# All subtractions for low parts put on VectorE, and a new model of the engines in the clock that orders a four-mixer encoder

## The chip, the cores and the metric

One core of one Trainium2 chip runs the whole program. The metric is device time in microseconds (us); lower is better. The engines are TensorE (PE in the profile, its weight loads PEld), VectorE (DVE), ScalarE (ACT), GpSimd (POOL) and SyncE (SP, which here only issues transfers).

## The reference

Two residual layers over 1024 tokens of width 1024. In each layer one input projection feeds four causal token mixers, each is gated and projected back, the four are merged by sigmoid gates, and an output projection closes the layer:

```python
h = _rmsnorm(x, norm_w)
p = h @ w_in                       # 1024 -> all inputs, gates of the four branches included
u_a = _rwkv7_branch(...)           # RWKV-7: state recurrence with a rank-one removal per token
u_b = _retention_branch(...)       # retention: chunked decay attention
u_c = _ssd_branch(...)             # Mamba-2 SSD: convolution, then chunked decay attention
u_d = _gdn_branch(...)             # gated DeltaNet: convolution, then a triangular solve per chunk
merged = sum(gates[:, :, b] * (u_b_ @ w_branch[b]) for b, u_b_ in enumerate((u_a, u_b, u_c, u_d)))
x = x + merged @ w_out
```

After the second layer comes a last RMSNorm. Everything is float32.

## The kernel before

The work goes in four passes: two layers, each over two halves of 512 tokens. Weights come in slabs of 128 x 512 values (912 in all). A product keeps float32 accuracy with TensorE's faster format `fp32r` by splitting both operands into a high part H (the value cast to `fp32r`) and a low part L (the value minus H): each block of a slab is used for H·H, H·L and L·H, so a slab of four blocks is 12 matmuls of 512 columns. The cast of a slab (`hl<-raw`, ACT or DVE) is made up to three slabs ahead of its use, and the subtraction (also `hl<-raw,hl`) up to two slabs ahead; `split` and `low` emit them, `prefetch` calls them when a slab is taken. The same subtraction gives the L parts of the normalised input (`hL`), of the branches' results (`u`, `acc`, `lo`) and of small operands of the RWKV-7 and DeltaNet units (`w`, `GE`, `GF`).

`subtract` decides which engine makes an L part:

```python
def sooner(self, a, b, n, what=""):
    ck = self.ck
    return ck.t[a] + ck.cost(a, what, n) <= ck.t[b] + ck.cost(b, what, n) + 0.8

def subtract(self, out, a, b):
    e = self.nc.gpsimd if self.sooner("gpsimd", "vector", int(np.prod(out.shape[1:]))) else self.nc.vector
    e.tensor_tensor(out, a, b, ALU.subtract)
```

Each pass runs 12 units (pieces of the mixers: `ret`, `gdn`, `ssd`, `rw`), every one a chain of short steps that go back and forth between PE and the other engines. Beside them runs the stream of big products (input projection, merges, gates, output projection), which needs nothing of the chains for most of its length. The program is one straight list of instructions, and each engine takes its own in the order in which they were emitted. That order is set when the program is built, by `Clock`, an estimate of when each engine gets to what is emitted: `Clock.cost` has a price for every instruction, `Clock.op` adds it after what the instruction reads or overwrites is over, and the loop in `mixers` emits a unit's next step as soon as the clock's PE time has reached the step's ready time, and otherwise a piece of the stream of products:

```python
now = ck.t["pe"]
for t in sorted(self.tasks, ...):
    if t.ready > now:
        continue
    ck.step = now
    r = next(t.gen, "end")             # emit one step of a unit
    ...
    t.ready = ck.step + ck.HAND        # the next step: after all this one emitted is over
    break
else:
    r = next(fill, "end") if more else None   # emit a piece of a product
```

So where the clock takes an engine for faster than it is, a unit's product stands too early in PE's queue, and PE, which takes its instructions in order, stands still there.

The chains that matter here are the inverses of unit lower triangular matrices (`inverse`, 12 per pass: 4 of `gdn`, 8 of `rw`). One inverse begins on DVE with the diagonal blocks (`invw<-GA,con` or `invw<-GE,con`, four instructions), a reduction and three or four instructions `GR<-invw,con`. Then PE spreads them (`m<-GR,con`, the first matmul of an inverse), DVE solves the small blocks in some twenty short dependent instructions (`invw<-m,invw`, `invw<-invw`, 4 to 64 elements), and five to eight rounds of PE and DVE double the blocks (`m<-invw,GA`, `m<-invw,GE`, `m<-invw`). The scores from which `GA` is made are `m<-w,w` and `m<-GE,w`. In the convolution (`ev_conv`, units `gdn` and `ssd`) DVE runs three instructions `cvy<-cvraw,par,cvy` and one `in<-cvraw,cvy` for each block of 128 channels.

Names in the profile: `g` are PSUM banks of the big products, `m` and `y` those of the units; `raw` and `hl` a slab as it comes and its H and L parts; `hH`/`hL`/`u` activations; `invw`, `GR`, `GA`, `GD`, `GE`, `GF`, `w` the units' working tiles; `rs` roots on POOL. All instructions of DVE, ACT and POOL have the line of the recording helper, L365 (L387 after the change), and PE has L438 for a matmul and L442 for a transpose (L465 and L469), so one goes by the tiles' names.

Of the kernel before, what the change touches and what calls it, by code (L numbers as in the profile page):

```python
# [16 lines left out]
P = 128  # L17
D = 1024
S = 1024
T = 512          # tokens per pass  # L20
NC = 4           # chunks per pass
C = 128          # tokens per chunk
# [5 lines left out]
# units in the order in which a pass runs them  # L28
# [3 lines left out]
# what a unit takes from the input projection, in the order of the products, with its place in memory; what has two  # L32
# places is 256 columns wide and has the tokens in the partitions
# [11 lines left out]
# The products of a pass in the order in which the tensor engine takes them, between the steps of the units.  # L45
# "out" is the output projection of the pass before, "norm" the normalisation of the input of the next pass;
# the last branch is merged in two steps, gates and projections.
# [4 lines left out]
# the first pass  # L52
# [10 lines left out]
# the others  # L63
# [36 lines left out]
def slabs_of(it):  # L100
    """The slabs of weights of an item of the plan, each of four blocks of 128 rows and 128 columns, or of two of
    128 rows and 256 columns."""
    if it[0] in ("sm", "lora", "out"):
        return [it + (e,) for e in range(2)]
    if it[0] == "in":
        return [("in",) + UNITS[it[1]] + (it[2], e) for e in range(2 * len(ROLES[UNITS[it[1]][0]][it[2]]))]
    if it[0] == "merge":
        b = BRANCH[it[1]]
        return [("gate", b, it[2], 0), ("gate", b, it[2], 1), ("proj", b, it[2])]
    b = BRANCH[MERGES[-1]]  # L110
    return {"gate": [("gate", b, it[-1], 0), ("gate", b, it[-1], 1)], "proj": [("proj", b, it[-1])], "norm": []}[it[0]]
# [7 lines left out]
def sequence(npass):  # L119
    """The items of the plan for all passes, each with its pass."""  # L120
# [32 lines left out]
# columns of the packed small parameters  # L153
# [10 lines left out]
def ssd_blk(idx, role):  # L164
    """Index of a 128-wide block of xbc."""
# [46 lines left out]
# constants: name -> (first column, width)  # L212
# [10 lines left out]
def make_consts():  # L223
# [42 lines left out]
    rope = np.stack([ct, st, ct * sc, st * sc])          # 4, P, S  # L266
# [4 lines left out]
class Clock:  # L271
    """An estimate, in microseconds, of when the engines get to what is emitted; it orders the steps."""
    HAND = 0.2       # from one engine to another

    def __init__(self):
        self.t = {e: 0.0 for e in ("pe", "vector", "scalar", "gpsimd", "dma")}
        self.slot, self.owner, self.written, self.read = {}, {}, {}, {}
        self.step = 0.0

    def place(self, tile, key):  # L280
        """The tile lies where the last one with this key lay."""
        self.slot[tile] = key
        self.owner[key] = tile

    def grains(self, ap):
        """Pieces of 128 elements of a tile's place which an operand touches; a bank of PSUM counts as one, as its
        users take turns."""
# [12 lines left out]
    def op(self, eng, outs, ins, cost):  # L300
        at = self.t[eng]
        gi, go = [g for a in ins for g in self.grains(a)], [g for a in outs for g in self.grains(a)]
        for g in gi:
            w = self.written.get(g)
            if w:
                at = max(at, w[0] + (0.13 if w[1] == eng else self.HAND))
        for g in go + [g for g in gi if g[1] < 0]:
            for d in (self.written, self.read):
                w = d.get(g)
                if w and w[1] != eng:  # L310
                    at = max(at, w[0] + self.HAND)
        end = self.wait(eng, at) + cost
        for g in gi:
# [10 lines left out]
    def settled(self, *aps):  # L324
        """When the last writes to these operands are over."""
# [6 lines left out]
    def cost(self, eng, name, n):  # L332
        if eng == "vector":
            return 0.07 + n * (0.52e-3 if name == "copy" else 1.04e-3)
        if eng == "scalar":
            return 0.1 + n * 0.83e-3
        return {"memset": 0.1 + n * 0.83e-3, "tensor_copy": 0.2 + n * 3.4e-3, "affine_select": 0.2 + n * 0.85e-3,
                "pow": 0.4 + n * 0.165}.get(name, 0.2 + n * 1.97e-3)


class Engine:
    """An engine whose instructions the clock sees."""
# [4 lines left out]
    def __getattr__(self, what):  # L347
        fn = getattr(self.real, what)

        def call(*a, **k):  # L350
# [8 lines left out]
            else:  # L359
                nm = "pow" if ALU.pow in a else what  # L360
                if what == "tensor_copy" and self.name == "vector" and not any(x.tensor.name.split("_")[0] in "mgy" for x in ops):
                    nm = "copy"
                self.clock.op(self.name, outs, [x for x in ops if not any(x is o for o in outs)],
                              self.clock.cost(self.name, nm, n))
# [11 lines left out]
def finish(gen):  # L376
    """What the generator returns, after all its steps."""
# [12 lines left out]
class Trunk:  # L390
# [12 lines left out]
    # ---------------------------------------------------------------- tiles  # L403
# [29 lines left out]
    # ---------------------------------------------------------------- tensor engine, with its time kept  # L433
    def mm(self, out, lhsT, rhs, **k):
        n, m = (int(np.prod(ap.shape[1:])) for ap in (rhs, lhsT))
        cost = (2 if m > 64 else 1.2) * max(n, m, 16) * 0.84e-3 if rhs.dtype == F32 else max(n, 64) * 0.42e-3
# [3 lines left out]
    def tr(self, out, in_, ident):  # L440
        self.ck.op("pe", [out], [in_], max(out.shape[-1], in_.shape[-1]) * 0.84e-3)
        self.nc.tensor.transpose(out, in_, ident)  # L442

    # ---------------------------------------------------------------- set-up
    def setup(self):
        nc = self.nc
        # schedule state
# [48 lines left out]
    def derive(self, l):  # L496
        """What follows from the parameters alone."""
# [14 lines left out]
    # ---------------------------------------------------------------- weights  # L512
# [4 lines left out]
    def prefetch(self, g):  # L517
        """Loads up to slab g + 5; H parts up to slab g + 3, L parts up to slab g + 2."""
# [4 lines left out]
    def split(self, high, low):  # L523
        """H parts of the slabs up to high, L parts of those up to low."""
# [25 lines left out]
    def flush(self):  # L550
        """The last steps of what takes the products out of PSUM."""
# [4 lines left out]
    def sooner(self, a, b, n, what=""):  # L556
        """Whether engine a is done sooner with an instruction over n elements than engine b."""
        ck = self.ck
        return ck.t[a] + ck.cost(a, what, n) <= ck.t[b] + ck.cost(b, what, n) + 0.8

    def subtract(self, out, a, b):
        e = self.nc.gpsimd if self.sooner("gpsimd", "vector", int(np.prod(out.shape[1:]))) else self.nc.vector
# [15 lines left out]
    def slab_gemm(self, rhs, evac):  # L578
        """The next slabs of weights, as H + L, against rhs, pairs of H and L of blocks of 128 rows."""
# [17 lines left out]
    def narrow_gemm(self, rhs, evac):  # L597
        """The like for 16 columns, which the slabs have twice: H and L parts side by side."""
# [13 lines left out]
    def wide_gemm(self, lhs, evac):  # L612
        """The like with the tokens in the partitions, for slabs of 256 columns; a bank has two chunks."""
# [23 lines left out]
    # ---------------------------------------------------------------- norm  # L637
# [3 lines left out]
    def squares(self, acc, k, x, tags=("w5", "w6")):  # L641
        """acc (+)= x^2"""
# [7 lines left out]
    def rms_rows(self, *accs, tag="w7"):  # L650
        """[P, T] tile with rsqrt(mean(x^2) + eps) of each token in every partition; accs have the squares' sums
        over the blocks of 128 features."""
# [20 lines left out]
    def wt(self, i):  # L673
        """A tile in the working memory of the units, free when none of them runs."""
# [50 lines left out]
    # ---------------------------------------------------------------- input blocks  # L725
    def ev_shift(self, ps, l, muix, mu, out, hf):
        """Token shift: out = t * (1 - mu) + previous(t) * mu."""
# [12 lines left out]
    def ev_conv(self, ps, l, cvix, wname, wix, bias, out, hf, done):  # L740
        """Causal convolution of four taps, then 2 * silu."""
# [26 lines left out]
    def ev_silu(self, ps, out):  # L768
        """out = 2 * silu(ps)."""
# [4 lines left out]
    def unit_input(self, l, hf, kind, idx, role, io):  # L774
        """One of the blocks of 128 columns of the input projection which a unit takes."""
# [43 lines left out]
    def small(self, l, hf):  # L819
        """dt, beta and alpha of every head: decays, their running sums and what follows from them."""  # L820
# [9 lines left out]
    def decays(self, l, hf, s):  # L830
# [17 lines left out]
        # log(1 + e) = 2 atanh(e / (2 + e))  # L848
# [33 lines left out]
    def lora(self, l, hf):  # L882
        """The narrow inputs of RWKV-7, with the H part in one half of the partitions and the L part in the other."""
# [15 lines left out]
    # ---------------------------------------------------------------- merge  # L899
    def h_gemm(self, evac, gemm=None):  # L900
        """The next slabs against the normalised input; at the start against what is not yet scaled."""
# [53 lines left out]
    # where the gates of the last branch wait: in working memory, and in the places of inputs  # L955
# [1055 lines left out]
```

## Time and profile before

| | before |
|---|---|
| time, median of 3 runs | 3782.73 us (3783.42, 3778.8, 3782.73) |
| span of the profiled execution | 3775.2 us |
| its own time | only the span is given; the runs lie 3.6 to 8.2 us above it |
| PE busy | 3577.6 us (95%) |
| DVE busy | 2543.6 us (67%) |
| POOL busy | 1790.6 us (47%) |
| ACT busy | 1401.4 us (37%) |
| transfers | 295.48 MB, mean 78 GB/s |

How to read it: the span runs from the first to the last instruction. A matmul's busy time is modelled and matmuls overlap, so PE's 95% isn't PE at its peak; what counts for PE is the time in which it stands still, what ended each of these waits, and the granted clock (1.0 is full speed). On the other engines idle time costs nothing by itself.

### The profile page before, as it was taken

The numbers are of one execution on the slowest core, as the hardware profiler recorded it, in microseconds if no ns is written. First come the engines' busy times: TensorE is split into PE (matmuls) and PEld (weight loads), VectorE is DVE, ScalarE is ACT, GpSimd is POOL, SyncE is SP. The second block draws the span as 40 slices with busy tenths as digits, with TensorE's granted clock in tenths as the row PEclk, the third lists the DMA queues.
The fourth block names the chain that finished last, engine by engine and source line by source line (L and its number), as shares of the span: only waits on it lengthen the run. The fifth ranks groups of instructions, "written<-read, shape, count | busy, mean of one in ns | idle before, by whom it ended". The sixth has DMA issues, their size and how long they took to land. (4 is left out here: it accounts for less than half of the span.)

```text
span 3775.2 us, 66152 instructions
## 1 busy us (share of the span) xinstructions
PE 3577.6 (95%) x24904; PEld 2864.7 (76%) x24904; DVE 2543.6 (67%) x5607; ACT 1401.4 (37%) x3121; POOL 1790.6 (47%) x1846
## 2 busy tenths in 40 slices
PE   7999999999999999999999999999999999999998
PEld 5777877777877787777787778777778778867777
DVE  6678666766577856567657775757665876675664
ACT  4433343333243334333324334433332433443333
POOL 4534554545453445445545445444454534454444
PEclk9999999999999999999999999999999999999999
DMA  3212222113322222212332222221243222221124
GB/s 121 72 59 65 73 72 61 52 60 114 124 76 79 65 73 68 61 54 71 113 126 75 71 73 70 62 64 55 71 125 113 86 64 68 70 65 58 57 76 148
DMA packets 162176, 295.48 MB, mean 78 GB/s; under 512 B 17984, under 2 KB 21440, under 8 KB 161856
## 3 DMA queue, kind: packets, MB, share of 16 engines
q1 hardware_dynamic: 150192, 271.22, 24.1%
q10 hardware_dynamic: 11664, 20.02, 1.6%
q8 instruction: 197, 3.23, 0.4%
q14 instruction: 123, 1.01, 0.1%
HBM read 280.69 MB, written 10.49 MB: 77 GB/s over the span
## 5 line engine op out<-in xcount | busy, mean ns | idle before, releaser
L438 PE MATMUL g<-hH,hl 128*128 128x512 f32 (+1 forms) x5176 | 1773.9, 415 | 8.4 <-DVE cvraw L365 4.9
L365 POOL TENSOR_TENSOR hl<-raw,hl 128x512 fp32r<-128x512 f32 x700 | 960.6, 1377 | 745.0 <-ACT hl L365 659.2
L438 PEld LDWEIGHTS g<-hH,hl 128*128 128x128 f32 (+1 forms) x5176 | 974.9, 191 | 240.5 <-issue 10.3
L438 PE MATMUL g<-hL,hl 128*128 128x512 f32 x2600 | 1040.8, 400 | 0.0
L365 ACT CAST hl<-raw 128x512 fp32r<-128x512 f32 x851 | 521.8, 618 | 684.4 <-PE g L438 270.0
L438 PE MATMUL g<-u,hl 128*128 128x512 f32 (+1 forms) x2112 | 608.9, 411 | 24.1 <-ACT hH L365 9.7
L438 PEld LDWEIGHTS g<-hL,hl 128*128 128x128 f32 x2600 | 496.8, 191 | 113.0 <-issue 8.6
L438 PEld LDWEIGHTS g<-u,hl 128*128 128x128 f32 (+1 forms) x2112 | 391.5, 191 | 122.3 <-ACT hH L365 12.2
L365 POOL TENSOR_TENSOR rs<-rs,mhalf 128x4 f32<-128x4 f32 (+2 forms) x80 | 106.5, 1331 | 401.5 <-DVE rs L365 401.2
L365 DVE SCALAR_TENSOR_TENSOR cvy<-cvraw,par,cvy 128x512 f32<-128x512 f32 x244 | 257.7, 1056 | 41.8 <-ACT cvy L365 30.4
L365 DVE TENSOR_TENSOR hl<-raw,hl 128x512 fp32r<-128x512 f32 x212 | 211.5, 1007 | 27.4 <-ACT hl L365 26.3
L438 PE MATMUL g<-hl,hH 128*128 128x256 f32 x1024 | 190.0, 285 | 2.7 <-DVE hl L365 2.7
L365 DVE TENSOR_TENSOR invw<-invw 128x4 f32<-128x4 f32 (+3 forms) x464 | 164.3, 354 | 15.9
L365 ACT COPY cvraw<-g 128x512 f32<-128x512 f32 (+1 forms) x160 | 93.5, 585 | 187.5 <-PE g L438 145.6
L438 PEld LDWEIGHTS g<-hl,hH 128*128 128x128 f32 x1024 | 160.3, 191 | 3.6 <-DVE hl L365 2.9
L365 POOL TENSOR_SCALAR_AFFINE_SELECT GA<-GA 128x512 f32<-128x512 f32 x128 | 85.2, 672 | 121.8 <-ACT GA L365 121.8
L365 ACT ACTIVATE cvraw<-cvy 128x512 f32<-128x512 f32 x80 | 50.2, 628 | 234.9 <-DVE cvy L365 217.2
L365 POOL TENSOR_TENSOR acc<-acc,tg 128x512 f32<-128x512 f32 x64 | 90.3, 1411 | 81.4 <-DVE tg L365 70.6
L438 PE MATMUL g<-hl,hL 128*128 128x256 f32 x512 | 125.6, 283 | 0.0
L438 PE MATMUL m<-w,w 64*128 64x256 f32 (+1 forms) x640 | 115.5, 312 | 1.3 <-ACT w L365 0.5
L365 ACT ACTIVATE tg<-g 128x512 f32<-128x512 f32 x100 | 59.6, 596 | 150.1 <-PE g L438 109.1
L365 ACT ACTIVATE in<-g 128x512 f32<-128x512 f32 x84 | 49.3, 597 | 169.2 <-PE g L438 169.2
(340 smaller groups left out, 5682.2 us busy)
## 6 DMA issues: line engine op xcount, KB each, us to landing
raw<-W SPq DMA_DIRECT2D x912, 256.0 KB, 2.6
w<-x ACTq DMA_DIRECT2D x32, 256.0 KB, 3.5
tg<-rope SPq DMA_DIRECT2D x16, 256.0 KB, 3.0
cvy<-rope SPq DMA_DIRECT2D x16, 256.0 KB, 3.4
w<-x SPq DMA_DIRECT2D x16, 256.0 KB, 4.4
x<-tg ACTq DMA_DIRECT2D x12, 256.0 KB, 2.1
x<-cvy ACTq DMA_DIRECT2D x12, 256.0 KB, 2.0
GA<-xT SPq DMA_DIRECT2D x8, 256.0 KB, 5.1
```

The source lines that it names most:

```text
L365: return fn(*a, **k)
L438: self.nc.tensor.matmul(out, lhsT, rhs, **k)
```

## The change

Three things change; tables of the order of products, tiles and arithmetic stay, and comments are dropped.

1. `subtract` always takes VectorE.
2. The clock knows a port that VectorE and GpSimd share: an instruction for which `ported` holds (all of GpSimd's that read, and on VectorE `tensor_tensor`, `scalar_tensor_tensor` and copies whose operands all lie in SBUF, and longer `tensor_scalar`) starts only when the port is free and holds it to its end. `sooner` looks at the port too.
3. Prices change: a `fp32r` matmul of 512 columns from 0.215 to 0.233 us, small float32 matmuls by their tile, GpSimd's copies and selections, a surcharge for `scalar_tensor_tensor` and for a sum written beside an activation.

```diff
-    def op(self, eng, outs, ins, cost):
+    def op(self, eng, outs, ins, cost, port=False):
...
+        if port:
+            at = max(at, self.port)
         end = self.wait(eng, at) + cost
+        if port:
+            self.port = end
...
-        return {"memset": 0.1 + n * 0.83e-3, "tensor_copy": 0.2 + n * 3.4e-3, "affine_select": 0.2 + n * 0.85e-3,
-                "pow": 0.4 + n * 0.165}.get(name, 0.2 + n * 1.97e-3)
+        return {"memset": 0.1 + n * 0.83e-3, "tensor_copy": 0.13 + n * 1e-3, "affine_select": 0.1 + n * 0.95e-3,
+                "pow": 0.4 + n * 0.15}.get(name, 0.2 + n * 1.97e-3)
+
+    def ported(self, eng, name, ins):
+        if eng == "scalar" or not ins or any(self.slot.get(x.tensor.name, ("",))[0] in ("m", "g", "y") for x in ins):
+            return False
+        return eng == "gpsimd" or name in ("tensor_tensor", "scalar_tensor_tensor", "tensor_copy", "copy") \
+            or (name == "tensor_scalar" and int(np.prod(ins[0].shape[1:])) >= 32)
+
+    def free(self, eng, port=False):
+        return max(self.t[eng], self.port) if port else self.t[eng]
...
+                if port and what == "scalar_tensor_tensor":
+                    c += n * 0.12e-3
+                if self.name == "scalar" and k.get("accum_out") is not None:
+                    c += 0.15
...
-        cost = (2 if m > 64 else 1.2) * max(n, m, 16) * 0.84e-3 if rhs.dtype == F32 else max(n, 64) * 0.42e-3
+        if rhs.dtype != F32:
+            cost = max(n, 128) * 0.456e-3
+        elif m <= 64:
+            cost = 0.03 if m <= 32 else 0.11 if n <= 64 else n * 1.7e-3
+        else:
+            cost = 2 * max(n, m) * 0.85e-3
...
-        return ck.t[a] + ck.cost(a, what, n) <= ck.t[b] + ck.cost(b, what, n) + 0.8
+        at = {e: ck.free(e, e != "scalar") + ck.cost(e, what, n) for e in (a, b)}
+        return at[a] <= at[b] + 0.8
...
-        e = self.nc.gpsimd if self.sooner("gpsimd", "vector", int(np.prod(out.shape[1:]))) else self.nc.vector
+        e = self.nc.vector
```

In the built program the counts are: PE 19362 matmuls before and now; DVE 5609 and 6514; POOL 1851 and 910; ACT 3044 and 3079; SP 1045 and 1045. From POOL to DVE go 940 subtractions: 700 of slabs (`hl<-raw,hl`, 912 of 912 are now on DVE), 86 others of 512 elements and 154 of 256, and one scaling at the end. 37 casts of slabs go from DVE to ACT.

First place: DVE's queue where the first group of the second `rw` unit of the first pass begins its inverse. `GD` to `GE` are the operands of another group's scores, `hl` are slabs. Before:

```order
L365 SCALAR_TENSOR_TENSOR GD_6_6252<-in_10_4896,par_67,w_7_5514 128x2x128
L365 TENSOR_TENSOR GD_6_6252<-in_10_4956,w_7_5514 128x2x128
L365 TENSOR_TENSOR GF_7_6259<-w_11_5736,GF_7_6259 128x256
L365 TENSOR_TENSOR GE_7_6258<-GD_6_6252,w_13_6257 128x512
L365 TENSOR_TENSOR invw_4_6268<-GA_7_6102,con_81 32x128 x4
L365 TENSOR_REDUCE invw_4_6268<-invw_4_6268 128x32
L365 TENSOR_TENSOR GR_6_6103<-invw_4_6268,con_81 128x64
```

Now:

```order
L387 TENSOR_TENSOR hl_6179<-raw_6092,hl_6179 128x512
L387 SCALAR_TENSOR_TENSOR GD_6_6252<-in_10_4876,par_67,w_7_5571 128x2x128
L387 TENSOR_TENSOR GD_6_6252<-in_10_4938,w_7_5571 128x2x128
L387 TENSOR_TENSOR w_15_6255<-w_13_5732,w_15_6255 128x256
L387 TENSOR_TENSOR w_12_6256<-w_9_5737,w_12_6256 128x256
L387 TENSOR_TENSOR GF_7_6259<-w_11_5739,GF_7_6259 128x256
L387 TENSOR_TENSOR GE_7_6258<-GD_6_6252,w_13_6257 128x512
L387 TENSOR_TENSOR invw_4_6268<-GA_7_6102,con_81 32x128 x4
L387 TENSOR_REDUCE invw_4_6268<-invw_4_6268 128x32
L387 TENSOR_TENSOR GR_6_6103<-invw_4_6268,con_81 128x64
```

The slab's and two `w` subtractions, which stood on POOL, now stand on DVE ahead of the inverse; from `GE` on the rows are the same.

Second place: PE's queue where the first `gdn` inverse of the second pass begins with `m<-GR,con` (128x480). `g` rows are the stream of products, `hl_` the slab. Before:

```order
L438 MATMUL g_10747<-hH_8995,hl_10639 128x512 x4
L438 MATMUL g_10747<-hH_8995,hl_10666 128x512
L438 MATMUL g_10747<-hL_8996,hl_10666 128x512
L438 MATMUL m_10782<-GR_10_10527,con_81 128x480
L438 MATMUL g_10747<-hH_8995,hl_10666 128x512
```

Now:

```order
L465 MATMUL g_10795<-hH_8995,hl_10738 128x512 x4
L465 MATMUL g_10839<-hH_8995,hl_10757 128x512
L465 MATMUL g_10839<-hL_8996,hl_10757 128x512
L465 MATMUL m_10847<-GR_10_10532,con_81 128x480
L465 MATMUL g_10839<-hH_8995,hl_10757 128x512
```

The inverse's first product has moved back in PE's queue by three slabs, 36 matmuls of 512 columns (`hl_10685` and `hl_10738` stand in between).

Third place: POOL's queue in the first pass, where an `rw` unit's state is carried from chunk to chunk (`sf`, `sh`). Before:

```order
L365 MEMSET sh_6848 128x128
L365 TENSOR_TENSOR sf_6885<-sh_6848,fc_5603 128x128
L365 TENSOR_TENSOR hl_6837<-raw_6744,hl_6837 128x512
L365 MEMSET sh_6916 128x128
L365 TENSOR_TENSOR rs_9_6929<-rs_9_6929,mhalf_89 128x4
L365 TENSOR_TENSOR hl_6899<-raw_6791,hl_6899 128x512
L365 TENSOR_TENSOR sf_6973<-sh_6916,fc_5603 128x128
```

Now:

```order
L387 TENSOR_TENSOR sf_6902<-sh_6278,fc_5651 128x128
L387 MEMSET sh_6944 128x128
L387 TENSOR_TENSOR sf_6965<-sh_6944,fc_5651 128x128
L387 MEMSET sh_6981 128x128
L387 TENSOR_TENSOR rs_9_6994<-rs_9_6994,mhalf_89 128x4
```

No subtraction is left on POOL; its other work stands as before.

More of the change, by code (lines that the diff above doesn't have):

```diff
@@ L273 @@
     HAND = 0.2
+    SAME = 0.13
     def __init__(self):
@@ L278, in __init__ @@
         self.step = 0.0
+        self.port = 0.0
     def place(self, tile, key):
@@ L305, in op @@
             if w:
-                at = max(at, w[0] + (0.13 if w[1] == eng else self.HAND))
+                at = max(at, w[0] + (self.SAME if w[1] == eng else self.HAND))
         for g in go + [g for g in gi if g[1] < 0]:
@@ L362, in call @@
                     nm = "copy"
-                self.clock.op(self.name, outs, [x for x in ops if not any(x is o for o in outs)],
-                              self.clock.cost(self.name, nm, n))
+                ins = [x for x in ops if not any(x is o for o in outs)]
+                c, port = self.clock.cost(self.name, nm, n), self.clock.ported(self.name, what, ins)
+                if port and what == "scalar_tensor_tensor":
+                    c += n * 0.12e-3
+                if self.name == "scalar" and k.get("accum_out") is not None:
+                    c += 0.15
+                self.clock.op(self.name, outs, ins, c, port)
             return fn(*a, **k)
@@ L440, in tr @@
     def tr(self, out, in_, ident):
-        self.ck.op("pe", [out], [in_], max(out.shape[-1], in_.shape[-1]) * 0.84e-3)
+        self.ck.op("pe", [out], [in_], max(out.shape[-1], in_.shape[-1]) * 0.86e-3)
         self.nc.tensor.transpose(out, in_, ident)
```

## Prediction

> **What bounds the kernel now.** I read the page's head first, then the waits of PE, then one long wait as a timeline, then the rows of the tiles in it. The page and the list of cores:
>
> ```profile
> span 3775.2 us, 66152 instructions
> PE 3577.6 (95%) x24904; PEld 2864.7 (76%) x24904; DVE 2543.6 (67%) x5607; ACT 1401.4 (37%) x3121; POOL 1790.6 (47%) x1846
> core 0: 3775.2 us, clock 0.978
> ```
>
> PE stands still for 3775.2 − 3577.6 = 198 us. The granted clock of 0.978 costs 3775.2 x 0.022 = 83 us more. The rest is matmul work that the change doesn't touch, so at most 281 us can go, and some of that belongs to the start and the end. Who ends PE's waits (us in total, times, longest):
>
> ```profile
> PE m L438 <- DVE invw L365: 77.3, 62, 2.7
> PE m L438 <- DVE GR L365: 13.8, 10, 3.6
> PE m L438 <- DVE GE L365: 12.9, 18, 1.5
> PE m L438 <- DVE stgdn L365: 11.0, 14, 1.9
> PE g L438 <- ACT hH L365: 9.7, 6, 2.4
> PE m L438 <- DVE yB L365: 8.9, 4, 3.4
> PE m L442 <- DVE GA L365: 6.3, 15, 1.1
> PE g L438 <- POOL hl L365: 2.3, 7, 0.5
> ```
>
> Steps of the units that DVE has not finished end most of it: the first four rows alone are 115.0 us. The slabs' L parts on POOL (last row) are no bottleneck themselves. Why DVE is late shows the timeline at the first place of the order (start, duration, engine; the bracket is the idle time before):
>
> ```profile
> 662.24 1.77 DVE L365 TENSOR_TENSOR GE<-GD,w 128x512 fp32r<-128x512 f32 x1
> 663.42 1.72 POOL L365 TENSOR_TENSOR hl<-raw,hl 128x512 fp32r<-128x512 f32 x1
> 663.94 2.61 DVE L365 TENSOR_TENSOR invw<-GA,con 32x128 f32<-32x128 f32 x4
> 664.07 0.39 PE L438 MATMUL m<-GE,w 64*128 64x256 f32 x1 [0.64 <-DVE GE L365]
> 665.55 0.39 PE L438 MATMUL g<-hL,hl 128*128 128x512 f32 x1
> 666.59 0.38 DVE L365 TENSOR_REDUCE invw<-invw 128x32 f32<-128x128 f32 x1
> 667.00 1.48 DVE L365 TENSOR_TENSOR GR<-invw,con 128x64 f32<-128x64 f32 x3
> 667.02 1.32 POOL L365 TENSOR_TENSOR hl<-raw,hl 128x512 fp32r<-128x512 f32 x1
> 668.62 0.45 PE L438 MATMUL m<-GR,con 128*128 128x112 f32 x2 [2.68 <-DVE invw L365]
> ```
>
> While a slab's subtraction runs on POOL, DVE's instructions with two inputs in SBUF stretch: four short ones take 2.61 us, three others 1.48 us. PE has run out of the products put ahead of `m<-GR,con` at 665.94 and waits 2.68 us. The tiles' rows (minimum, median, maximum in ns; then two groups with busy time and mean) say the same for all passes:
>
> ```profile
> L365 DVE TENSOR_TENSOR invw<-GA,con x128: 268/289/1362, 562.5 to 3636.5; 32x128 f32<-32x128 f32 x128
> L365 DVE TENSOR_TENSOR GR<-invw,con x160: 160/218/1357, 190.9 to 3637.5; 128x64 f32<-128x64 f32 x48, 128x32 f32<-128x32 f32 x48, 128x16 f32<-128x16 f32 x32, 128x256 f32<-128x256 f32 x16
> L365 DVE TENSOR_TENSOR invw<-invw x464: 166/168/1349, 198.4 to 3644.8; 128x4 f32<-128x4 f32 x87, 128x8 f32<-128x8 f32 x41, 128x16 f32<-128x16 f32 x23, 128x32 f32<-128x32 f32 x4
> L365 DVE TENSOR_TENSOR invw<-invw 128x4 f32<-128x4 f32 (+3 forms) x464 | 164.3, 354 | 15.9
> L365 DVE SCALAR_TENSOR_TENSOR cvy<-cvraw,par,cvy x244: 750/752/1710, 138.0 to 3243.6; 128x512 f32<-128x512 f32 x122
> L365 DVE SCALAR_TENSOR_TENSOR cvy<-cvraw,par,cvy 128x512 f32<-128x512 f32 x244 | 257.7, 1056 | 41.8 <-ACT cvy L365 30.4
> L365 POOL TENSOR_TENSOR hl<-raw,hl x700: 1256/1297/2267, 4.7 to 3752.0; 128x512 fp32r<-128x512 f32 x175
> ```
>
> Medians are clean, means and maxima are not: the longest `invw<-invw` is 168 ns plus about one POOL subtraction. In the solve of one inverse the loss is 464 x (354 − 168) ns / 48 inverses = 1.8 us, near the long waits at `m<-invw`.
>
> **The change part by part.** What leaves POOL is 15 groups. The largest and the smallest of them, ACT's cast of a slab, three instructions that follow each other on DVE (from the timeline), and the longest undisturbed run of products (from the chain of work that ended last):
>
> ```profile
> L365 POOL TENSOR_TENSOR hl<-raw,hl 128x512 fp32r<-128x512 f32 x700 | 960.6, 1377 | 745.0 <-ACT hl L365 659.2 <-DVE hl L365 52.7 <-PE m L438 16.6
> L365 POOL TENSOR_TENSOR lo<-tg,u 128x512 fp32r<-128x512 f32 x1 | 1.3, 1309 | 1.3 <-ACT u L365 1.3
> L365 ACT CAST hl<-raw 128x512 fp32r<-128x512 f32 x851 | 521.8, 618 | 684.4 <-PE g L438 270.0 <-issue 121.7 <-DMA raw<-W 109.6
> 742.36 0.41 DVE L365 TENSOR_TENSOR GD<-in,w 128x256 f32<-128x256 f32 x1
> 742.69 0.68 DVE L365 TENSOR_TENSOR hl<-raw,hl 128x512 fp32r<-128x512 f32 x1
> 743.29 0.15 DVE L365 TENSOR_TENSOR invw<-m,invw 128x4 f32<-128x4 f32 x1
> 3414.33 25.25 PE g L438 x108
> ```
>
> All 15 together are 1215 us, so POOL keeps about 575 us, 32% of its time. On DVE a subtraction occupies the queue from its start to the next start: 743.29 − 742.69 = 0.60 us for 512 elements, 742.69 − 742.36 = 0.33 us for 256. So DVE takes on 786 x 0.60 + 154 x 0.33 = 522 us; the 37 casts that leave it only lower that. It gets back, from the two rows of excess shown above, 244 x (1056 − 752) + 464 x (354 − 168) ns = 160 us, of which POOL's 68% is 109 us, and more from rows not shown. A subtraction also waits for its cast, and on DVE everything behind it waits along:
>
> ```profile
> L365 DVE TENSOR_TENSOR hl<-raw,hl 128x512 fp32r<-128x512 f32 x212 | 211.5, 1007 | 27.4 <-ACT hl L365 26.3
> ```
>
> The 212 already on DVE stood 26.3 us for ACT, 0.12 us each (on POOL 659.2 us, where nothing urgent was behind); 700 more make 87 us.
>
> The terms for PE, against the span:
>
> A. The four rows of 115.0 us. At 668.6 the clean chain is 4 x 0.29 + 0.38 + 3 x 0.22 = 2.2 us from 663.94 and ends at 666.1, 0.2 us after PE's products: the wait of 2.68 us shrinks to that. The slab's and the two `w` subtractions, now ahead of `GE` on DVE, cost 1.26 us there, but delay the scores `m<-GE,w` and the inverse alike. At the second place `m<-GR,con` also stands 36 matmuls of 25.25/108 = 0.234 us, 8.4 us, further back, for a wait of at most 3.6 us. As 32% of POOL's time stays to collide with, I take two thirds of the row: −77 us. Ends: 0 (the subtractions on DVE are as much in the way as POOL was) and −115.
>
> B. The other rows of DVE (`yB`, `GA`: 15.2 us): half, −8; ends 0 and −15. ACT's rows and the start stay.
>
> C. The clock. The stretch right behind the wait at 668.6 (length, then busy time of PE, PEld, DVE, ACT and POOL; the granted clock stands third from the end):
>
> ```profile
> 669.10:672.50 3.40, 3.40 (x13) 2.39 (x14) 2.85 (x17) 1.10 (x2) 0.00 (x0) 0.50 0.28 77
> ```
>
> After a wait of 2.68 us PE gets half speed for 3.4 us, which costs 1.7 us more. The 83 us shrink with the waits, by (77 + 8)/198: −36 us; ends 0 and −65. The Trainium skill, "TensorE: Matmul & The Clock Gate", section "HAM oscillation — how this bites in real kernels", puts the limit at idle gaps over about 3.4 us, by which this term would be near 0 and the sum −65. The trace disagrees: 2.68 us was enough, and the row decides.
>
> D. What gets in the way anew. The subtractions and their waits take (522 + 87)/3775 = 16% of DVE's time. The order has 48 inverses with 7 or 9 groups of products, 400 in all; if each meets half a subtraction (0.30 us) with that probability and nothing covers it, that is 400 x 0.16 x 0.30 = 19 us: +20. Ends: 0, and 400 x 0.30 = +120 if each one meets one.
>
> Costed at nothing: the casts on ACT (37 x 0.618 = 23 us; ACT is 37% busy and sits 684 us idle before such casts; a slab is cast three slabs of 12 x 0.234 = 2.8 us ahead; without that cover 23 us). A slab's L part is due two slabs, 5.6 us, ahead; if DVE's queue is longer than that, PE waits on `hl`, and the slab's `raw` buffer comes free later, so that SP issues the next load later: between 0 and +20, I take 0, since the longest block, a convolution's, is 3 x 0.75 us. POOL's roots `rs` and states `sf` lose the subtractions ahead of them; DVE has room for these waits, so no gain is counted.
>
> Sum: −77 − 8 − 36 + 20 = −101 us. The profiled span lies 7.5 us below the median of the runs; 3782.7 − 101 = 3682 us.
>
> **The rivals.** *Slower, because DVE becomes the bound.* Three stretches of 95 us (PE, PEld, DVE, ACT, POOL busy), then the part of slabs' tiles in the first:
>
> ```profile
> 1995.00:2090.00 95.00, 89.27 (x488) 71.10 (x487) 80.72 (x163) 43.39 (x118) 54.30 (x48) 0.96 0.27 82
> 2945.00:3040.00 95.00, 85.67 (x559) 66.91 (x558) 81.57 (x193) 42.23 (x110) 45.55 (x46) 0.98 0.25 81
> 1900.00:1995.00 95.00, 94.60 (x493) 77.74 (x492) 51.17 (x102) 27.39 (x57) 39.49 (x30) 1.00 0.37 117
> 1995.00:2090.00 95.00, 80.61 (x324) 60.47 (x323) 4.89 (x3) 15.88 (x26) 34.37 (x24) 0.96 0.27 82
> ```
>
> In the convolutions DVE is already at 81 of 95 us; 24 subtractions more are +14.4, which is full unless the contention goes. Between the second and third row PE loses 8.9 us for 30.4 us more of DVE, 0.29 per us. If DVE ends 300 us busier over all (522 less twice the relief counted above), that is +87: 3870 us. It decides from the point at which a convolution stretch stays above some 90 of 95 us. Against it: the same rows' POOL time falls by 34 of 54 us, and `cvy` alone loses 0.3 us a piece in contention. *Little, because the places only change.* The port is held by DVE's own subtractions instead of POOL's, and the order gains a third of A and C: about −40, 3740 us. The Trainium skill, "Perfetto Trace Analysis", section "Optimizing Scalar/DVE Operations", says that moving work between GpSimd and DVE might not help, as they share a port. Against it stand 1.297 us on POOL for 0.60 on DVE. *No change*, if D eats all of A to C: 3783. *Nearly all goes*: A, B and C at their ends, D 0: −195, 3588 us.
>
> **How the numbers follow.** The forecast case (3635 to 3730) 0.45; little (3730 to 3775) 0.22; nearly all (3560 to 3635) 0.15; no change 0.05; slower 0.13. The skill's rule on the clock has 0.03 of the forecast's chance, and its 3718 lies inside. A change within 0.2% (7.6 us) can't be told from none; so faster 0.82, same 0.05, slower 0.13. For 8 in 10 the range goes from 3575 to 3785: it leaves out nearly all of slower and the lowest tail of the gain.
>
> **What the profile after would show.** POOL near 575 us, `hl<-raw,hl` x912 on DVE with a mean near 0.75 us, `invw<-invw` well under 354 ns, `cvy` under 900: contention gone. DVE at 2700 to 2950 us: D and the relief. PE's waits for `invw`, `GR`, `GE`, `stgdn` under 50 us in all and a clock of 0.985 or more: A and C. I am wrong if PE's waits for `hl`, `hH` or `u` grow by tens of us, or if DVE's contention with what stays on POOL (roots, selections, sums) keeps the inverses as long as they are.

## The result, and the profile after

| | before | changed kernel |
|---|---|---|
| median of the runs (lowest to highest) | 3783.07 us (3778.8 to 3791.84, 4 runs) | 3702.70 us (3700.13 to 3705.72, 4 runs) |
| ratio, 95% interval | | 0.978 [0.9762, 0.9798] |
| profiled execution: span | 3775.2 us | 3703.7 us |
| PE busy, PE standing still | 3577.6, 197.6 us | 3553.5, 150.2 us |

The kernel became 80 us faster; 101 had been forecast. The profiled execution of before was one of the quicker ones and that of the changed kernel the slowest of its four, so the two traces differ by 71.5 us. The head of the page, after:

```profile
span 3703.7 us, 65695 instructions
PE 3553.5 (96%) x24904; PEld 2854.5 (77%) x24904; DVE 2595.0 (70%) x6512; ACT 1427.2 (39%) x3156; POOL 600.5 (16%) x905
```

And the list of cores, with the granted clock (0.978 before):

```profile
core 0: 3703.7 us, clock 0.981
```

POOL lost 1190 us of work, DVE won 905 instructions and yet only 51 us. The reason stands in the groups of DVE (busy time, mean ns of one, then the idle time ahead of them):

```profile
L387 DVE TENSOR_TENSOR hl<-raw,hl 128x512 fp32r<-128x512 f32 x912 | 667.8, 740 | 42.4 <-ACT hl L387 39.7
L387 DVE SCALAR_TENSOR_TENSOR cvy<-cvraw,par,cvy 128x512 f32<-128x512 f32 x244 | 186.7, 765 | 56.2 <-ACT cvy L387 46.8 <-issue 0.5
L387 DVE TENSOR_TENSOR invw<-invw 128x4 f32<-128x4 f32 (+3 forms) x464 | 83.6, 180 | 15.9
```

and in the tile's row (minimum, median, maximum in ns):

```profile
L387 DVE TENSOR_TENSOR invw<-invw x464: 166/168/721, 190.7 to 3574.6; 128x4 f32<-128x4 f32 x87, 128x8 f32<-128x8 f32 x41, 128x16 f32<-128x16 f32 x23, 128x32 f32<-128x32 f32 x4
```

The means have come down to the medians: 354 to 180 ns in the inverses, 1056 to 765 ns in the convolutions, 1007 to 740 ns in the slabs' own subtraction. The longest `invw<-invw` is 721 ns instead of 1349. That DVE itself was no slower before is shown by a neighbour of these instructions in the same chain, which has one of its two inputs in PSUM (`m`) and not in SBUF. Its row before and after:

```profile
L365 DVE TENSOR_TENSOR invw<-m,invw x480: 122/164/292, 198.2 to 3644.6; 128x4 f32<-128x4 f32 x88, 128x16 f32<-128x16 f32 x40, 128x64 f32<-128x64 f32 x24, 128x128 f32<-128x128 f32 x8
L387 DVE TENSOR_TENSOR invw<-m,invw x480: 122/164/293, 190.5 to 3574.4; 128x4 f32<-128x4 f32 x88, 128x16 f32<-128x16 f32 x40, 128x64 f32<-128x64 f32 x24, 128x128 f32<-128x128 f32 x8
```

It never stretched: its longest is 292 ns with POOL busy for 47% of the time and 293 with 16%. The same steps as at the first place of the order, in the timeline of after:

```profile
638.09 0.68 DVE L387 TENSOR_TENSOR GE<-GD,w 128x512 fp32r<-128x512 f32 x1
638.69 1.17 DVE L387 TENSOR_TENSOR invw<-GA,con 32x128 f32<-32x128 f32 x4
640.32 0.41 DVE L387 TENSOR_TENSOR GR<-invw,con 128x64 f32<-128x64 f32 x3
641.00 0.37 PE L465 MATMUL m<-GR,con 128*128 128x112 f32 x2
```

The four short ones take 1.17 us (2.61 before), the three others 0.41 (1.48), and PE takes `m<-GR,con` without a wait (2.68 before). The rest of the gain's story is in PE's waits (total us, times, longest):

```profile
PE g L465 <- DVE hl L387: 48.1, 33, 7.4
PE m L465 <- DVE invw L387: 18.6, 25, 3.6
PE m L465 <- ACT w L387: 17.1, 6, 3.4
PE g L465 <- DVE cvraw L387: 11.7, 7, 2.4
PE m L465 <- DVE yC L387: 8.7, 3, 3.0
PE m L465 <- DVE GE L387: 2.4, 6, 0.6
PE m L465 <- DVE GR L387: 2.0, 3, 0.7
PE m L469 <- DVE yB L387: 1.9, 2, 1.7
```

The four rows that led before, 115.0 us, are 23.0 us (`stgdn` has no row any more). At the top stands a wait for slabs' L parts. It had been 7.0 us: the 2.3 us of POOL's row and this one:

```profile
PE g L438 <- DVE hl L365: 4.7, 3, 2.7
```

The longest wait for `hl` after, in the timeline:

```profile
1101.18 0.40 PE L465 MATMUL g<-acc,hl 128*128 128x512 f32 x1
1103.07 0.68 ACT L387 ACTIVATE cvy<-g,par 128x512 f32<-128x512 f32 x1
1103.78 3.03 DVE L387 SCALAR_TENSOR_TENSOR cvy<-cvraw,par,cvy 128x512 f32<-128x512 f32 x3 [1.13 <-ACT cvy L387]
1106.90 0.63 ACT L387 ACTIVATE cvraw<-cvy 128x512 f32<-128x512 f32 x1 [3.16 <-DVE cvy L387]
1107.44 1.12 ACT L387 CAST hl<-raw 128x512 fp32r<-128x512 f32 x2
1107.64 0.69 DVE L387 SCALAR_TENSOR_TENSOR in<-cvraw,cvy 128x512 f32<-128x512 f32 x1 [0.83 <-ACT cvraw L387]
1108.25 1.29 DVE L387 TENSOR_TENSOR hl<-raw,hl 128x512 fp32r<-128x512 f32 x2
1108.99 1.22 PE L465 MATMUL g<-u,hl 128*128 128x512 f32 x2 [7.40 <-DVE hl L387]
```

A convolution goes from ACT to DVE, back to ACT and to DVE again, each waiting for the other (1.13, 3.16 and 0.83 us in the brackets). The cast of the next slab stands behind it in ACT's queue and the subtraction behind it in DVE's. Both engines are idle at times, but neither can take the slab first, and PE has no products left at 1101.6. What that wait costs beyond itself is shown by the granted clock (third from the end; ahead of it length and busy time of PE, PEld, DVE, ACT, POOL):

```profile
1104.95:1108.90 3.95, 0.00 (x0) 0.00 (x0) 3.05 (x6) 1.66 (x3) 0.33 (x2) 0.50 0.01 2
1109.00:1115.00 6.00, 6.00 (x80) 4.90 (x81) 4.18 (x13) 0.62 (x1) 0.00 (x0) 0.50 0.63 217
1115.00:1122.00 7.00, 7.00 (x59) 5.06 (x59) 6.49 (x25) 1.71 (x4) 1.67 (x5) 0.99 0.19 52
```

After a wait of 7.40 us PE works 6.0 us at half speed, where the wait of 2.68 us before had been followed by 3.4.

### The profile page after: what moved, and what is told of

Read it like the earlier page. It is cut to its first block, busy times and chain, and to the rows that moved or that the text cites. A ratio compares the mean times of both kernels' runs of the same rounds, so it can differ in the third digit from the quotient of the medians.

```text
span 3703.7 us, 65695 instructions
## 1 busy us (share of the span) xinstructions
PE 3553.5 (96%) x24904; PEld 2854.5 (77%) x24904; DVE 2595.0 (70%) x6512; ACT 1427.2 (39%) x3156; POOL 600.5 (16%) x905
## 5 line engine op out<-in xcount | busy, mean ns | idle before, releaser
L465 PEld LDWEIGHTS g<-hH,hl 128*128 128x128 f32 (+1 forms) x5176 | 957.8, 189 | 255.0 <-DVE hl L387 27.2
L387 ACT CAST hl<-raw 128x512 fp32r<-128x512 f32 x888 | 546.6, 619 | 727.9 <-PE g L465 373.9
L387 DVE TENSOR_TENSOR hl<-raw,hl 128x512 fp32r<-128x512 f32 x912 | 667.8, 740 | 42.4 <-ACT hl L387 39.7
L387 DVE SCALAR_TENSOR_TENSOR cvy<-cvraw,par,cvy 128x512 f32<-128x512 f32 x244 | 186.7, 765 | 56.2 <-ACT cvy L387 46.8
L465 PEld LDWEIGHTS g<-hl,hH 128*128 128x128 f32 x1024 | 162.9, 193 | 1.9 <-DVE hl L387 1.2
L465 PE MATMUL m<-w,w 64*128 64x256 f32 (+1 forms) x640 | 118.5, 319 | 17.1 <-ACT w L387 17.1
L465 PEld LDWEIGHTS m<-w,w 64*128 64x128 f32 (+1 forms) x640 | 90.8, 204 | 37.9 <-ACT w L387 18.4
L387 POOL COPY GR<-invw 32x128 f32<-32x128 f32 x192 | 65.7, 342 | 232.3 <-DVE invw L387 226.0
L465 PEld LDWEIGHTS g<-hl,hL 128*128 128x128 f32 x512 | 100.0, 195 | 4.3 <-DVE hL L387 3.5
```

What stands on the lines that cost most here:

```text
L387: return fn(*a, **k)
L465: self.nc.tensor.matmul(out, lhsT, rhs, **k)
```

## The experiments

All kernels were timed in three rounds beside the kernel before (medians 3780 to 3784 us). "Theory" and "rivals" in the expectations are those of the prediction and of the questions that the result left: is the gain the move's or the clock's, what makes the new waits for `hl`, and what do the clock's new parts do.

**The clock without the move, and the move without the clock.** The first is the changed kernel with the old choice of engine, the second the kernel before with the new one:

```diff
# e1_clock_only, against the changed kernel
-        e = self.nc.vector
+        e = self.nc.gpsimd if self.sooner("gpsimd", "vector", int(np.prod(out.shape[1:]))) else self.nc.vector
# e2_move_only, against the kernel before
-        e = self.nc.gpsimd if self.sooner("gpsimd", "vector", int(np.prod(out.shape[1:]))) else self.nc.vector
+        e = self.nc.vector
```

> The changed kernel, but the engine of a subtraction is chosen by the clock again (856 of 912 slab subtractions then stand on POOL, 700 did before). Theory 'contention' (the gain is that the subtractions leave the port): the collisions come back, invw<-invw on DVE has a mean of 330 ns or more, PE's waits for DVE invw, GR, GE and stgdn are over 90 us together, time 3740 to 3800 us. Rival 'order' (the new clock alone makes the gain, the place of the subtractions is neutral): time within 10 us of the changed kernel's 3703 us.

> The kernel before with its old clock, all subtractions on VectorE. Theory 'contention': invw<-invw falls under 200 ns on the mean, the four DVE rows under 50 us, time 3690 to 3740 us. Rival 'order': 3775 us or more, since the old clock takes PE for faster than it is and knows nothing of the port.

Measured: `e1_clock_only` 3952.3 us, ratio 1.0447 [1.0425, 1.0469]; `e2_move_only` 3699.5 us, ratio 0.978 [0.9764, 0.9796]. Groups of the first:

```profile
L387 POOL TENSOR_TENSOR hl<-raw,hl 128x512 fp32r<-128x512 f32 x856 | 1151.7, 1355 | 645.9 <-ACT hl L387 580.5 <-issue 39.0 <-DMA raw<-W 11.8
L387 DVE TENSOR_TENSOR invw<-invw 128x4 f32<-128x4 f32 (+3 forms) x464 | 153.4, 331 | 15.9
```

its waits of PE:

```profile
PE m L465 <- DVE invw L387: 61.0, 48, 3.0
PE m L465 <- DVE GR L387: 37.7, 15, 7.6
```

the group of the inverses in the second:

```profile
L365 DVE TENSOR_TENSOR invw<-invw 128x4 f32<-128x4 f32 (+3 forms) x464 | 93.7, 202 | 15.9
```

and its waits of PE:

```profile
PE m L438 <- DVE invw L365: 26.3, 17, 4.8
PE g L438 <- DVE hl L365: 24.0, 34, 3.5
PE m L438 <- DVE GR L365: 12.1, 3, 4.0
```

The move alone gives the whole gain, within its interval, at a time that theory 'contention' had foreseen; with the old clock the inverses' mean falls from 354 to 202 ns (just over the 200 of the theory) and the four rows from 115.0 to 42.8 us (`GE` has 4.4 of them, `stgdn` none). With the subtractions on POOL the stretched inverses and their waits are back, and the new clock, which then puts 856 slabs there instead of 700, makes the kernel 171 us slower than before, far outside both ranges. So the new clock brings no gain of its own where POOL is loaded; how much of the 171 us is its order and how much the 156 further slabs, this run does not separate.

**The clock's parts.** With the move made, the new clock moves the time from 3699.5 to 3702.7, nothing. Either it does nothing, or its parts cancel. One kernel leaves the port out (with it go the surcharge of 0.06 us for `scalar_tensor_tensor` and the port in `sooner`), one lets an instruction wait only if it would overlap the port's last holder, and one takes from the new prices only that of the `fp32r` matmuls, on the kernel before with the move:

```diff
# e4_no_port_term, against the changed kernel
     def ported(self, eng, name, ins):
+        return False
# e6_port_interval, against the changed kernel
...
-        if port:
-            at = max(at, self.port)
+        if port and at + cost > self.port[0]:
+            at = max(at, self.port[1])
         end = self.wait(eng, at) + cost
-        if port:
-            self.port = end
+        if port and end > self.port[1]:
+            self.port = (end - cost, end)
...
# e7_move_mm_price, against e2_move_only
-        cost = (2 if m > 64 else 1.2) * max(n, m, 16) * 0.84e-3 if rhs.dtype == F32 else max(n, 64) * 0.42e-3
+        cost = (2 if m > 64 else 1.2) * max(n, m, 16) * 0.84e-3 if rhs.dtype == F32 else max(n, 128) * 0.456e-3
```

> The changed kernel with the clock's port term off (an instruction never waits for the port in the estimate); subtractions on VectorE and new prices stay. Theory 'contention': little is left on POOL to collide with, so the term is worth little, 3690 to 3715 us. Rival 'order': the term is what puts the steps right; without it 3735 us or more.

> The changed kernel, whose clock keeps the port term but as an interval: an instruction waits for the port only if it would overlap the last one that held it, and not if it can run before that one begins. Theory 'phantom' (the port term costs because a holder that is itself still to come, waiting for PE, pushes back work that on the chip runs before it): the time comes near the kernel without the term, 3635 to 3665 us. Rival 'any port delay' (the estimate gets worse by every port wait, real or not): 3690 us or more.

> The kernel before with all subtractions on VectorE and one new price, that of the fp32r matmul (512 columns 0.233 instead of 0.215 us); no port term, other prices old. Theory 'matmul price' (the 56 us that the new prices are worth come from PE's own price, since PE's time decides when a step is emitted): 3640 to 3665 us. Rival 'small prices' (they come from the small matmuls and from GpSimd's prices): 3685 to 3705 us, as with the move alone.

Measured: `e4_no_port_term` 3643.6 us, ratio 0.9633 [0.9618, 0.9647]; `e6_port_interval` 3664.6 us, 0.9682 [0.9656, 0.9707]; `e7_move_mm_price` 3665.5 us, 0.9683 [0.9661, 0.9705]. The head of the page without the port term:

```profile
PE 3523.8 (97%) x24904; PEld 2832.3 (78%) x24904; DVE 2609.0 (72%) x6505; ACT 1428.7 (39%) x3163; POOL 621.3 (17%) x911
```

the list of cores:

```profile
core 0: 3641.2 us, clock 0.993
```

the waits of PE:

```profile
PE g L466 <- DVE hl L388: 42.2, 38, 4.6
PE m L466 <- DVE GR L388: 14.0, 8, 7.1
PE m L466 <- DVE invw L388: 8.7, 27, 0.6
```

and the group of the inverses:

```profile
L388 DVE TENSOR_TENSOR invw<-invw 128x4 f32<-128x4 f32 (+3 forms) x464 | 86.4, 186 | 15.9
```

Of the forecasts, `e4_no_port_term` is under both ranges, so neither the theory nor its rival saw that the term costs time; the other two come out near the ends of their theories' ranges (3665). The parts do cancel: the matmul price takes 34 us off (3699.5 to 3665.5; the trace's 0.234 us a matmul is the new price's 0.233, the old one was 0.215), the other prices perhaps 22 more, and the port term with its surcharge gives 59 back. The engines' work is nearly the same with and without the term, and the inverses' mean is 186 against 180 ns, so no contention comes back when the clock stops minding the port. What differs is where PE stands still: 117.4 us instead of 150.2, with 10 waits of 2 us or more instead of 26. And the clock falls less often: its records have 10 stretches at half speed instead of 25, and its mean is 0.993 for 0.981. Over the span that would be 3641.2 x 0.007 = 25 us lost instead of 70, but in part of this time PE stands still anyway; its busy time fell by 29.7 us. The interval form recovers 38 of the 59 us, in one order. That speaks for phantom waits: the clock books the port in the order in which the steps are written, so that an instruction which could run in an earlier gap of the port is put behind its last holder. The other 21 us it does not explain (the surcharge, which this kernel keeps, may be in them).

**Is 59 us more than the luck of an order?** Any change of the clock makes another order of thousands of steps. So the clock's hand-over time between engines was set to 0.22 and to 0.18 us, with the port term and without:

```diff
-    HAND = 0.2
+    HAND = 0.22    # or 0.18
```

> The changed kernel with the clock's hand-over between engines at 0.22 us instead of 0.20, port term kept: another order of the same work, at a guess of the clock that is as good. Theory 'port term': the 59 us between the changed kernel (3702.7) and the one without the port term (3643.6) belong to the term, so this stays with the port-term kernels: 3685 to 3720 us. Rival 'luck of the order': the steps' places scatter the time by some 30 us whatever the term, so that this may well come out under 3670 or above 3735.

> The changed kernel with the hand-over at 0.18 us, port term kept. Theory 'port term': 3685 to 3720 us. Rival 'luck of the order': anywhere from 3640 to 3740, so that the four kernels with changed hand-over do not fall into two groups by the port term.

> No port term, the hand-over at 0.22 us. Theory 'port term': 3630 to 3665 us, PE's waits for hl near 40 us. Rival 'luck of the order': 3643.6 was a lucky draw, and this comes out above 3675.

> No port term, the hand-over at 0.18 us. Theory 'port term': 3630 to 3665 us. Rival 'luck of the order': above 3675.

| hand-over in the clock | with the port term | without |
|---|---|---|
| 0.22 us | 3693.5 us, 0.9763 [0.9737, 0.9789] | 3638.9 us, 0.9623 [0.9597, 0.9649] |
| 0.20 us | 3702.7 us, 0.978 [0.9762, 0.9798] | 3643.6 us, 0.9633 [0.9618, 0.9647] |
| 0.18 us | 3681.3 us, 0.9732 [0.9705, 0.9759] | 3654.8 us, 0.9663 [0.9633, 0.9693] |

Another guess moves the time by up to 21 us, and one of the four, 3681.3, lies 4 us under the range that the theory gave; but the groups stay 26 us apart (3681.3 to 3654.8). The port term, with its surcharge, costs 47 us on average (3692.5 against 3645.8). What differs by 10 or 20 us between two single orders, as in the other prices' 22 and the rest of 21 above, is within that luck, and its cause is not shown. The 34 us of the matmul price are more than any of these moves, but rest on one pair of orders that was not shaken so. `e12_noport_hand22` is the fastest kernel measured, though not distinct from `e4_no_port_term`; both beat the changed kernel by about 1.6%.

**The waits for `hl`.** If they come from the queue on DVE, L parts made three slabs ahead instead of two should end them (after slab 60; with the port term and without):

```diff
-        self.split(min(g + 3, tot - 1), min(g + 2, tot - 1))
+        self.split(min(g + 3, tot - 1), min(g + (3 if g > 60 else 2), tot - 1))
```

> The changed kernel with a slab's L part emitted three slabs ahead of its use and not two (from the 61st slab on). Theory 'queue' (PE waits 48 us for hl because the subtraction stands in DVE's queue behind chains and convolutions for longer than the lead of 5.6 us): PE's wait for DVE hl falls under 15 us, time 3645 to 3680 us. Rival 'source' (the subtraction is late because its cast on ACT or the slab's load is late): the wait stays over 35 us, time 3690 to 3715 us.

> The changed kernel without the port term, and with a slab's L part three slabs ahead (from the 61st slab on). Theory 'queue': PE's wait for DVE hl, 42 us with a lead of two, falls under 12 us and most of it is kept, 3600 to 3630 us. Rival 'handed on' (as with the port term, the wait moves to the chains behind the subtractions): the hl wait falls, other waits grow by as much, 3635 to 3655 us.

Measured: `e3_lead3` 3691.5 us, ratio 0.9764 [0.9748, 0.978]; `e8_no_port_lead3` 3652.2 us, 0.965 [0.9628, 0.9672]. PE's waits in the first:

```profile
PE m L465 <- DVE invw L387: 29.5, 35, 2.8
PE m L469 <- DVE yB L387: 13.8, 8, 2.8
PE g L465 <- ACT hl L387: 12.0, 3, 4.0
PE g L465 <- DVE hl L387: 3.5, 2, 2.8
```

and DVE's group of the subtractions:

```profile
L387 DVE TENSOR_TENSOR hl<-raw,hl 128x512 fp32r<-128x512 f32 x912 | 662.1, 730 | 168.6 <-ACT hl L387 162.9
```

The waits for `hl` fall from 48.1 to 3.5 us (without the port term from 42.2 to 5.5), so it is the queue. The time hardly moves: −11 us in one pair, +8.5 in the other, both inside the luck of an order, and theory 'queue' misses both times. The wait is handed on, as the rival of that name said. A subtraction written one slab earlier stands next to its cast, DVE stops for ACT 162.9 us in all instead of 39.7, and the steps behind it in DVE's queue come later: PE's waits for `invw` rise from 18.6 to 29.5, for `yB` from 1.9 to 13.8, for the casts to 12.0.

**POOL as a relief.** Without the port term, slabs whose subtraction DVE would reach more than 6 us behind PE by the clock go to GpSimd (143 of 912):

```diff
-        e = self.nc.vector
+        ck = self.ck
+        late = ck.t["vector"] > ck.t["pe"] + 6.0 and int(np.prod(out.shape[1:])) == 4 * P
+        e = self.nc.gpsimd if late else self.nc.vector
```

> The changed kernel without the port term, and a slab's subtraction goes to GpSimd where the clock has VectorE more than 6 us ahead of PE (143 of 912). Theory 'contention': even these collide with DVE's chains, invw<-invw rises above 200 ns on the mean; the hl wait falls under 20 us; in all 3630 to 3670 us. Rival 'relief' (POOL is idle there, so it's free): 3600 to 3630 us.

Measured: 3704.1 us, ratio 0.9785 [0.9763, 0.9807], 60 us more than `e4_no_port_term` and outside both ranges. PE's waits:

```profile
PE g L466 <- POOL hl L388: 40.0, 16, 5.3
PE m L466 <- DVE invw L388: 35.2, 48, 3.3
```

and the groups on POOL and DVE:

```profile
L388 POOL TENSOR_TENSOR hl<-raw,hl 128x512 fp32r<-128x512 f32 x143 | 201.7, 1416 | 300.3 <-ACT hl L388 261.1 <-PE m L466 17.4 <-DVE invw L388 13.0
L388 DVE TENSOR_TENSOR invw<-invw 128x4 f32<-128x4 f32 (+3 forms) x464 | 115.1, 248 | 15.9
```

The waits for L parts are not relieved: 40.0 us for POOL, where one takes 1.42 us, and 1.9 for DVE, against the 42.2 of `e4_no_port_term`. What is new is that the inverses stretch again, 186 to 248 ns, although POOL is busy for only 23% of the time, and PE's waits for `invw` go from 8.7 to 35.2 us. The likely reason, not tested by itself, is that the rule picks DVE's busiest moments, in which a collision is most in the way. So the move pays for the last 143 slabs as it did for the first 700.

## Why the prediction was right, and where it was off

**Term A** (−77) held, and more than held: the four rows fell by 92.0 us. Its two reasons can be told apart. The contention went with the move alone (`e2_move_only`, old clock: 93.7 us of `invw<-invw` instead of 164.3), and the four rows came down to 42.8 us. The new clock's order took them on to 23.0, but nothing off the time (3702.7 against 3699.5 us), as the waits for `hl` went from 24.0 to 48.1. So the clock's part in A, which I had counted, is there in the rows and is paid back in others. Nor do these rows make the kernel without the port term faster: they are 25.0 us there.

**Term B** (−8): both rows, 15.2 us, are gone, at its end of −15 (a second row of `yB`, at other matmuls, stood at 1.7 and stands at 1.9). But `yC` rose from 1.0 to 8.7.

**Term C** (−36) failed in its size: 83 us lost to the clock became 3703.7 x 0.019 = 70, that is −13. I had let it shrink with the sum of the waits, but it goes by the long ones. Of PE's waits in the two traces, those under 2 us fell from 141 to 80, those of 2 us or more only from 32 to 26, and the stretches at half speed in the clock's records from 37 to 25 (from 164 to 141 us of the span). In the kernel without the port term 10 waits of 2 us or more are left, and 10 stretches. The 83 us were also too high a price to begin with, since PE stands still in part of the half-speed time: it worked in 143 of the 164 us, and in 113 of the 141 after, so that 71 us were lost before and 56 after. The Trainium skill, "TensorE: Matmul & The Clock Gate", section "HAM oscillation — how this bites in real kernels", would have no wait under about 3.4 us count. The 1.7 us behind the wait of 2.68 us before are against that. The three waits of 7.3 to 7.4 us after, which are what its rule is about, cost 7 of the 56 us.

**Term D and what was costed at nothing** is the step that failed. The waits for L parts were put between 0 and +20 us, taken as 0, on the ground that two slabs' lead, 5.6 us, is longer than the longest block of 3 x 0.75 us. They cost 48.1 − 7.0 = +41. The block is not three instructions but a chain between two queues with a wait at each turn: at 1101 to 1109 its first step on ACT begins at 1103.07 and the subtraction behind it at 1108.25, 5.2 us later, and the cast on ACT at 1107.44 was nearly as late. Two more of the 33 waits show the same rows (7.29 and 7.41 us), and three of 2.8 to 3.0 us stand behind three `cvy`; these six are 30.9 of the 48.1 us. The move brought about 17 of the +41 us (24.0 with the old clock), the new order the rest. Together with `ACT w` (0.5 to 17.1) and the smaller rows, less those that fell, it comes to more than the forecast allows: PE's idle time fell by 47.4 although A and B took 107, that is +60, where D had +20.

The sum on the traces: −92 − 15 (A, B), −13 (C), +60 (D and what was costed at nothing) = −60; with −11 us of PE's busy time that the clock's mean doesn't cover and that I can't assign, the 71.5 us. That the forecast of 101 came as near as it did is in part luck: A and B brought 22 us more than was forecast, C and D together 63 us less.

**The rivals.** *Slower*: it was to decide at 90 of 95 us of DVE in a convolution stretch. The same two stretches of the profile, after (length, busy time of PE, PEld, DVE, ACT, POOL):

```profile
1995.00:2090.00 95.00, 84.40 (x606) 67.20 (x605) 71.64 (x213) 35.91 (x100) 12.39 (x20) 0.96 0.24 70
2945.00:3040.00 95.00, 93.43 (x713) 74.30 (x713) 72.45 (x227) 31.95 (x74) 10.86 (x21) 0.98 0.23 69
```

DVE is at 72 of 95, less than the 81 of before, with all subtractions on it (the work in them has shifted by some tens of us). My 2700 to 2950 us for DVE was too high, since the relief was undercounted: 2543.6 + 522 − 2595.0 = 471 us less than the sum, against 160 counted in two rows. These two gave 81 + 71 = 152; the slabs' own 212 gave 212 x 0.267 = 57 more, the 37 casts that left some 20, and the rest lies in rows that I had not summed: the durations of all groups that run equally often in both traces fell by 363 us, 152 of it in the two rows. *Little*: the Trainium skill, "Perfetto Trace Analysis", section "Optimizing Scalar/DVE Operations", says that moving work between GpSimd and DVE might not help. Here it did: 940 instructions moved to DVE gave −82 us in `e2_move_only`. Nearer to the trace is the Trainium skill, "SBUF — State Buffer", section "Who interferes with whom": a DVE instruction with two inputs in SBUF contends with one of GpSimd that reads SBUF. The rows agree: with two inputs in SBUF the maximum was 1349 ns for a clean 168, nearly a whole POOL subtraction more, and with one of them in PSUM 292 ns. *Nearly all goes* at 3588 us was not reached, but `e12_noport_hand22`, another kernel, lies at the edge of its range with 3638.9.

Of the signs named beforehand POOL (600.5 for 575 us), `hl` (740 ns), `invw<-invw`, `cvy` and the four rows came as told; DVE's total and the clock (0.981, not 0.985) did not; and the sign for being wrong, `hl` growing by tens of us, came as well, without turning the sum.

## What to carry to other kernels

Two engines that slow each other are judged by the mean against the median of their short instructions, and the relief has to be summed over all rows of the slowed engine, the moved work's own among them: here DVE's total rose by a tenth of the 522 us moved onto it. A lead in slabs is no cover against a chain that goes to and fro between two in-order queues; add its waits, not its instructions. In a kernel whose order comes from a model, correct the price of the commonest instruction first (34 us here, in one pair of orders), and test a new term of the model by leaving it out and by shaking another constant: after the move the port term modelled a contention that was nearly gone, and cost 47 us on the mean of three pairs.

## What was not expected of the hardware

Half speed comes in whole pieces. In the clock's records of both traces each stretch at half speed, but for the one at the program's end, lasts 3.41 us or two or three times that, and the number of pieces does not simply follow the wait ahead of it. Before, a wait of 2.68 us is followed by 3.41 us (669.12 to 672.54) and one of 1.53 us by 10.24 (832.96 to 843.20). After, waits of 7.29 and 7.41 us have 6.83 us each. The stretch at the wait of 7.40 us is 10.24 us long (1104.94 to 1115.18) and begins while PE stands idle, 3.4 us after its last matmul ended; PE works in 6.2 us of it.
